# A decoder step on Trainium2: half of the fourth sequence's pages asked by ScalarE among the units, two tiles of x normed and turned one unit sooner

## The chip, the cores and the metric

The kernel runs on one core of one Trainium2 chip. The core's engines have instruction queues of their own: TensorE (PE in the profile) multiplies and transposes, VectorE (DVE) and ScalarE (ACT) work on tiles, GpSimd (POOL) does a little of the same, and SyncE (SP) here only asks for transfers. SP, ACT and POOL each ask for DMA transfers ("ask" in this document: the instruction that starts a transfer; "land": the moment its data is there). The metric is device microseconds of one execution, lower is better; the kernel before took 1262.57 us (median of three runs, 1260.37 to 1264.19).

## What is computed

One inference step of a one-layer decoder: forgetting attention (FoX) beside native sparse attention (NSA), gates, an output projection and an MLP, for a prompt of 512 tokens and for eight sequences of eight new tokens, each with a past of 2048 tokens in paged caches. The past of a sequence is 16 pages of 128 tokens, and a page table says where each lies. The change touches the part of NSA that compresses the past: raw keys and values of blocks of tokens go through a small MLP.

```python
def compress_blocks(x, pos, w1, w2):
    b, n = x.shape[:2]
    n_chunk = n // CMP_STRIDE
    xc = x[:, :n_chunk * CMP_STRIDE].reshape(b, n_chunk, CMP_STRIDE, NSA_GROUPS, HEAD_DIM)
    pos = pos.reshape(2, CMP_STRIDE, 1, HEAD_DIM)
    w1 = w1.reshape(2, CMP_STRIDE, HEAD_DIM, CMP_HIDDEN)
    lead = jnp.einsum('bncgd,cdh->bngh', xc + pos[0], w1[0])
    trail = jnp.einsum('bncgd,cdh->bngh', xc + pos[1], w1[1])
    return jnp.einsum('bngh,hd->bngd', jax.nn.silu(lead[:, :-1] + trail[:, 1:]), w2)
```

`x` here is a sequence's raw keys or values out of `cache_nsa_kv`. The change also moves the first step of the layer itself, `h = rms_norm(x, norm1_g) * (1 + sc1) + sh1`, for the first two tiles of 128 prompt tokens.

## The kernel before, in words

The change lies in `first_stage` (L509), the first 180 us or so of the step. It walks through 40 units. A unit is (sequences, `j` of 4, key or value): units 0 to 7 belong to sequence 0 alone, 8 to 15 to sequence 1 alone, 16 to 23 to sequences 2 and 3 together, 24 to 31 to 4 and 5, 32 to 39 to 6 and 7. A unit of one sequence is 256 columns wide, one of two is 512.

What a unit does: `cmp_order` copies a quarter of the sequence's pages (`cpg`) into another order (`ro`) on DVE, once for a key unit and the value unit behind it. The pages of a sequence lie in one tile, each spread over 16 of its 128 partitions and one half of their columns, so a `ro` copy (L115), which takes all partitions and both halves, reads all 16 pages, and the first one of a sequence can't start before the last page has landed. `rows_turn` turns `ro` on PE into `ct` (L83, four transposes for a sequence), and `split` brings `ct` back in two parts: `xh` by ACT (L112) and the remainder `xl` by DVE (L131). `cmp_hidden` is the matmuls `hid` on PE (L77), from `xh` and `xl` and the weights. The loop issues the turns of unit u+1 ahead of the matmuls of unit u; the order of PE's turns and matmuls is a fixed chain (`link`). Behind the matmuls of unit u follows whatever stands in `todo[u]`.

What stands in `todo` near the change: `norm(k)` squares tile k of x on ACT (`sq`), sums, and scales x on DVE (`norm_scaled`); `turned(k)`, two units later, turns the scaled tile on PE in two halves of four transposes (`nt`) and copies them into `hf`, one half by ACT and one by DVE. The constants' turns and the bias matmuls stand at units 10 and 12. x tiles are loaded by POOL into two buffers, the ada weights (`wada`, 1 MB each) by POOL too, from unit 13 on.

Who asks for the pages: `cmp_pages` asks for a sequence's pages on the queue named, through `by_page`: it reads eight entries of the page table into registers (L162), then issues eight asks of 128 KB each (L155), in the order 0, 4, 1, 5 and so on. SP asks for half of sequence 0 and ACT for the other half, SP then for all of 1, 2 and 3 ahead of the units, and for 4 to 7 out of `todo[8]`, `[14]`, `[20]` and `[22]`. Each ask is ordered behind the one before on its queue (`dma`), so the queue of an engine is first in, first out. `cpg` has four buffers, so sequence 4's pages go into the room of sequence 0.

The scheduler orders each engine's instructions by what they depend on. `pinned` and `behind` fix a piece of work behind the last `xh` copy and the last `xl` subtraction issued so far.

Of the kernel before, what the change touches and what calls it, by code (L numbers as in the profile page):

```python
# [45 lines left out]
class Step:  # L46
# [386 lines left out]

        self.cpg[b] = pe.tile([P, 2, 8, 256], F32, tag="cpg", bufs=4, name=f"cpg{b}")

    def cmp_pages(self, eng, b, pages=slice(0, 16), toks=slice(0, 8)):
        def load(p, n):
            page = self.I["cache_nsa_kv"][0, bass.ds(n, 1)].rearrange("o (q c) e g d -> (o q) c (e g d)", q=16)
            self.dma(eng, self.cpg[b].rearrange("(q p) h c e -> p q h c e", p=8)[p % 8, :, p // 8, toks],
                     page[:, toks, 0:256])  # L440

        self.by_page(eng, b, pages, load, 8, (0, 4, 1, 5, 2, 6, 3, 7))

    def cmp_order(self, pl, u):

# [63 lines left out]
    def first_stage(self, pl, pe, hf):  # L509
# [7 lines left out]
        def load_x():  # L517
            k = len(xs)
            xs.append(pe.tile([P, D], F32, tag="x", bufs=2, name=f"x{k}"))
            self.dma("gpsimd", xs[k][:TILES[k][1]], self.x_rows(k))  # L520

        def norm(k):
            with self.tc.issue_after(self.last_high):
                self.norm_scaled(xs[k], 0, k, xs[k], pl.tile([P, D], BF16, tag="csx", name=f"sq{k}"))

        def turned(k):
            t0, m = TILES[k]
            for h in range(2):
                self.copy(hf[:, 4 * h:4 * h + 4, t0:t0 + m], self.norm_turned(xs[k], 0, k, h))

        def behind():
            both = ExitStack()
            for i in (self.last_high, self.splits[-1]):
                both.enter_context(self.tc.issue_after(i))
            return both

        def pinned(f):
            def g():
                with behind():
                    f()  # L540
            return g
# [18 lines left out]
        self.constants()  # L560
        self.late_constants()
        self.cmp_pages("sync", 2)
        self.cmp_pages("sync", 3)

        ada, ends = [4, 0, 5, 1, 6, 2, 7, 3], {}
        todo = {u: [] for u in range(40)}
# [2 lines left out]
        todo[18] += [pinned(self.cmp_second_half)]  # L569
        todo[10] += [self.constants_turned, self.ada_turned, lambda: ends.update(b=self.cmp_bias(pe))]  # L570
        todo[12] += [lambda: self.cmp_bias_end(ends["b"])]
        for k, u in enumerate((12, 14, 17, 19, 23)):
            todo[u - 2] += [lambda k=k: norm(k)]
            todo[u] += [lambda k=k: turned(k)]
        pages = lambda b: lambda: (self.cmp_tile(pe, b), self.cmp_pages("sync", b))
        wada = lambda k: lambda: self.ada_first_load(pe, ada[k])
        def asked():
# [3 lines left out]
            with self.tc.issue_after(g.ins):  # L581
                load_x()

        todo[3] += [asked]
        todo[5] += [asked]
        todo[8] += [pages(4)]
# [1603 lines left out]
```

## Time and profile before

| | before |
|---|---|
| runs | 1262.57 us median (1260.37 to 1264.19) |
| profiled execution, its time | 1260.9 us |
| its span, first to last instruction | 1259.1 us |
| mean granted TensorE clock | 0.985 |
| up to the first turn of a page, at 18.0 us | PE idle |
| 18.0 to 172.0, the units | PE busy 145.0 of 154.0 us |
| 172.0 to 180.0, end of the units to the projection `z` | PE busy 6.3 of 8.0 us |
| behind 180.0 | PE busy 1049.3 of 1079.1 us |

The profile is of one execution; its times are microseconds from the first instruction. "Busy" is the union of an engine's compute instructions. A row of the timeline or of the chain begins with the start and the duration, then the engine, the line of the kernel, the operation, its result and source by the program's names with shapes, and in brackets the idle time before it and what ended it. A row of the windows shows for a stretch its length, the busy time and the number of instructions of PE, of PE's weight loads, of DVE, ACT and POOL, then the granted TensorE clock, the busy share of the DMA engines and GB/s. A row of the waits has the engine, what it waited to do, what it waited for, then the total, the number of times and the longest. "SPq" is SP's own instruction queue.

### The profile page before, as it was taken

How to read it: one execution, taken by the hardware profiler on the slowest of the kernel's cores; microseconds unless marked ns; L12 is line 12 of the kernel's file. 1: busy time of each engine (PE TensorE's matmuls, PEld its weight loads, DVE VectorE, ACT ScalarE, POOL GpSimd, SP SyncE). 2: the span in 40 equal slices, each digit the busy share in tenths (PEclk: the TensorE clock that was granted, in tenths of full speed). 3: DMA queues.
4: the chain of work that ended last, by engine and by line, in shares of the span. 5: the costliest groups of instructions: out<-in, count | busy, mean ns of one | idle time of the engine just before them, and what ended most of it. 6: DMA issues, size and time to landing. Idle time of an engine off the chain costs nothing.

```text
span 1259.1 us, 24790 instructions
## 1 busy us (share of the span) xinstructions
PE 1200.7 (95%) x9475; PEld 1030.0 (82%) x9475; DVE 695.4 (55%) x1893; ACT 509.4 (40%) x1136; POOL 130.3 (10%) x139
## 2 busy tenths in 40 slices
PE   4799999999999999999899998979999999999998
PEld 3787779999666656666899998979989889898896
DVE  3777775686788845655533345664233333434545
ACT  2444453444777744444422223254413123132230
POOL 2110000001211210000200000002102011020110
PEclk9999999999999899999999999999999999999999
DMA  9897337795766469885843324024304223142202
GB/s 208 230 250 200 109 97 249 249 320 177 252 222 206 146 201 321 254 272 179 223 115 85 85 84 131 4 68 134 101 34 134 68 68 100 39 129 68 67 18 75
DMA packets 170201, 188.11 MB, mean 149 GB/s; under 512 B 16185, under 2 KB 149762, under 8 KB 167906
## 3 DMA queue, kind: packets, MB, share of 16 engines
q1 hardware_dynamic: 157890, 167.13, 43.6%
q0 software_dynamic: 6880, 16.25, 4.5%
q10 hardware_dynamic: 5312, 3.15, 1.1%
q8 instruction: 75, 1.23, 0.4%
q14 instruction: 44, 0.36, 0.1%
HBM read 176.48 MB, written 30.90 MB: 165 GB/s over the span
## 4 chain that ended last, share of the span: by engine, by line
PE 83%; DVE 6%; DMA 4%; ACT 2%; SPq 2%; issue 1%; DVEq 0%; ACTq 0%
PE dn L77 17%; PE up L77 16%; PE z L77 9%; PE mg L77 8%; PE hid L77 5%; PE br L77 4%; PE ss L77 4%; PE wo L77 3%; SPq L155 2%; PE k L83 2%; DMA cpg<-in_cache_nsa_kv 2%; PE so L77 2%; PE ct L83 2%; PE ada L77 2%; PE sp L83 1%
## 5 line engine op out<-in xcount | busy, mean ns | idle before, releaser
L77 PE MATMUL z<-winh,h 128*128 128x264 f32 (+1 forms) x576 | 112.7, 289 | 1.9 <-DVE h L767 1.7
L1979 POOL TENSOR_TENSOR u<-u 128x576 f32<-128x576 f32 x32 | 54.7, 1711 | 428.7 <-ACT u L112 336.9
L77 PEld LDWEIGHTS z<-winh,h 128*128 128x128 f32 x576 | 93.0, 192 | 4.1 <-DVE h L767 2.9
L77 PE MATMUL z<-winl,h 128*128 128x264 f32 (+1 forms) x320 | 88.7, 286 | 0.0
L100 DVE TENSOR_TENSOR acc<-acc,dn 128x512 f32<-128x512 f32 x60 | 39.8, 686 | 77.4 <-PE dn L77 77.4
L77 PE MATMUL mg<-hH,wmh 128*128 128x288 f32 x256 | 76.6, 300 | 2.4 <-ACT wmh L112 2.4
L77 PE MATMUL mg<-hH,wml 128*128 128x288 f32 x256 | 75.8, 297 | 0.9 <-DVE wml L131 0.9
L77 PE MATMUL mg<-hL,wmh 128*128 128x288 f32 x256 | 72.6, 294 | 0.0
L112 ACT ACTIVATE xh<-ct 128x256 fp32r<-128x256 f32 x128 | 48.0, 384 | 57.9 <-PE ct L83 35.5
L767 DVE TENSOR_TENSOR u<-u,u 128x512 fp32r<-128x512 f32 x64 | 27.4, 469 | 63.0 <-ACT u L112 62.9
L77 PEld LDWEIGHTS z<-winl,h 128*128 128x128 f32 x320 | 61.2, 192 | 0.0
L131 DVE TENSOR_TENSOR xl<-ct,xh 128x256 fp32r<-128x256 f32 x128 | 51.4, 421 | 17.6 <-ACT xh L112 15.6
L83 PE MATMUL ct<-identF,ro 128*128 128x128 f32 x256 | 37.3, 286 | 20.5 <-DVE ro L115 19.8
L131 DVE TENSOR_TENSOR wml<-wmr,wmh 128x1024 fp32r<-128x1024 f32 x16 | 19.6, 1225 | 65.6 <-ACT wmh L112 65.6
L77 PEld LDWEIGHTS mg<-hH,wmh 128*128 128x128 f32 x256 | 48.6, 190 | 2.8 <-ACT wmh L112 2.7
L83 PEld LDWEIGHTS ct<-identF,ro 128*128 128x128 f32 x256 | 30.5, 149 | 23.8 <-DVE ro L115 18.4
L77 PEld LDWEIGHTS mg<-hH,wml 128*128 128x128 f32 x256 | 49.1, 192 | 1.1 <-DVE wml L131 1.1
L112 ACT ACTIVATE u<-up 128x256 f32<-128x256 f32 (+1 forms) x96 | 27.7, 325 | 50.9 <-PE up L77 50.9
L77 PEld LDWEIGHTS mg<-hL,wmh 128*128 128x128 f32 x256 | 47.1, 188 | 0.1
L77 PE MATMUL hid<-xh,w1hlv 128*128 128x512 f32 (+1 forms) x160 | 45.2, 369 | 0.5 <-ACT xh L112 0.4
L77 PE MATMUL hid<-xh,w1hlk 128*128 128x512 f32 (+1 forms) x160 | 45.0, 369 | 0.1
L112 ACT ACTIVATE u<-u 128x576 fp32r<-128x576 f32 x32 | 21.9, 686 | 44.2 <-POOL u L1979 44.2
(950 smaller groups left out, 3596.5 us busy)
## 6 DMA issues: line engine op xcount, KB each, us to landing
adw<-in_w_ada SPq DMA_DIRECT2D x16, 1024.0 KB
foxD<-in_cache_fox_kv SPq DMA_DIRECT2D x128, 128.0 KB
wur<-in_w_up SPq DMA_DIRECT2D x32, 512.0 KB
wdr<-in_w_down SPq DMA_DIRECT2D x32, 512.0 KB
cpg<-in_cache_nsa_kv SPq DMA_DIRECT2D x120, 128.0 KB
fr<-foxD SPq DMA_DIRECT2D x28, 512.0 KB
sr<-in_cache_nsa_kv SPq DMA_DIRECT2D x112, 128.0 KB
wada<-in_w_ada POOLq DMA_DIRECT2D x8, 1024.0 KB, 6.6
```

The source lines that it names most:

```text
L77: ins = self.nc.tensor.matmul(out, a, b, start=start, stop=stop, skip_group_check=True)
L83: ins = self.nc.tensor.transpose(out, in_, self.identF[:n, :n])
L100: self.nc.vector.tensor_tensor(out, a, b, op=op)
L112: return self.nc.scalar.activation(out, in_, f, **kw)
L131: self.splits.append((eng or self.nc.vector).tensor_tensor(l, x, h.bitcast(F32), op=OP.subtract).ins)
L155: self.issued[eng] = getattr(self.nc, eng).dma_start(out, in_).ins
L767: (eng or self.nc.vector).tensor_tensor(h2[:, o:o + n], x[:, i:i + n], h2[:, i:i + n].bitcast(F32), op=OP.subtract)
L1979: nc.gpsimd.tensor_tensor(u[j], u[j], u[j], op=OP.mult)
```

## The change

`cmp_pages` gets a parameter `step`, the number of table entries read at a time, with the old order of asks for 8 and the plain order otherwise. SP asks ahead of the units only for pages 0 to 7 of sequence 3 (the fourth). Pages 8 to 15 are asked by ACT, two each out of `todo[7]`, `[9]`, `[11]` and `[13]`, each pair with a table read of its own, and pinned behind the latest `xh` and `xl`. `norm` and `turned` of tiles 0 and 1 move from units 10/12 and 12/14 to 9/11 and 11/13.

```diff
-    def cmp_pages(self, eng, b, pages=slice(0, 16), toks=slice(0, 8)):
+    def cmp_pages(self, eng, b, pages=slice(0, 16), toks=slice(0, 8), step=8):
...
-        self.by_page(eng, b, pages, load, 8, (0, 4, 1, 5, 2, 6, 3, 7))
+        self.by_page(eng, b, pages, load, step, (0, 4, 1, 5, 2, 6, 3, 7) if step == 8 else None)
...
         self.cmp_pages("sync", 2)
-        self.cmp_pages("sync", 3)
+        self.cmp_pages("sync", 3, slice(0, 8))
...
-        for k, u in enumerate((12, 14, 17, 19, 23)):
+        for k, u in enumerate((11, 13, 17, 19, 23)):
             todo[u - 2] += [lambda k=k: norm(k)]
             todo[u] += [lambda k=k: turned(k)]
...
+        for k, u in enumerate((7, 9, 11, 13)):
+            todo[u] += [pinned(lambda k=k: self.cmp_pages("scalar", 3, slice(8 + 2 * k, 10 + 2 * k), step=2))]
         todo[3] += [asked]
```

In the built program ACT's four pairs stand behind the `xh` copies of units 8, 10, 12 and 14. The program's transfers between HBM and the core that SP and ACT ask for share eight completion counters in rotation.

## The prediction

> **What bounds the kernel now.** I read the page first, then who waited for whom on TensorE (PE), then the chain of waits around the longest wait inside the first stage, then the stretches of the clock.
>
> ```profile
> span 1259.1 us, 24790 instructions
> PE 1200.7 (95%) x9475; PEld 1030.0 (82%) x9475; DVE 695.4 (55%) x1893; ACT 509.4 (40%) x1136; POOL 130.3 (10%) x139
> ```
>
> ```profile
> PE nt L83 <- DVE x L104: 5.1, 1, 5.1
> PE z L77 <- DVE h L767: 1.7, 1, 1.7
> ```
>
> PE is busy for 95% of the span, so a change is worth what it takes from, or adds to, PE's idle time. In the stage that is edited one wait stands out: 5.1 us before the turns (transposes) of x tile 1.
>
> ```profile
> 54.62 5.03 DMA cpg<-in_cache_nsa_kv
> ...
> 60.64 0.69 DVE ro L115
> ...
> 62.72 1.97 PE nt L83 x8
> 64.68 1.71 PE ct L83 x8
> ```
>
> The chain gives the reason. The last of the 32 pages that SP asks for sequences 2 and 3 is asked at 54.62 and lands 5.03 us later. VectorE (DVE) stands in its program order at the reordering copy `ro` of that page, so the scaling of x tile 1 stands behind it until 62.7, and PE, done with its units, waits for that.
>
> ```profile
> 58.56:61.98 3.42, 0.00 (x0) 0.00 (x0) 2.10 (x7) 0.52 (x1) 0.00 (x0) 1.00 1.02 314
> 61.98:65.39 3.41, 2.67 (x13) 2.68 (x14) 1.35 (x3) 0.60 (x1) 0.41 (x1) 0.50 1.09 254
> 65.39:68.80 3.41, 3.41 (x18) 3.41 (x17) 1.63 (x5) 2.46 (x6) 1.04 (x2) 0.50 0.92 270
> ...
> 178.03:181.44 3.41, 1.59 (x8) 1.16 (x9) 3.35 (x9) 3.41 (x7) 0.76 (x3) 1.00 0.26 100
> 181.44:184.85 3.41, 3.41 (x15) 3.07 (x14) 3.41 (x11) 1.34 (x3) 0.00 (x0) 0.50 0.97 234
> ```
>
> The wait costs more than itself. After a stretch without a matmul the granted clock (third number from the end) is 0.50 for two stretches, 61.98 to 68.80; PE runs again from 62.72, so 6.08 us pass at half speed, a loss of 3.04. The wait and its tail together cost 8.1 us.
>
> **The change, part by part.** (1) SP asks for 8 pages fewer ahead of sequence 4. (2) ScalarE (ACT) asks for those 8 in four pairs, behind the copies of units 8, 10, 12 and 14, each pair with a read of the page table. (3) Tiles 0 and 1 are normed and turned one unit sooner. The number of copies, turns and matmuls stays. In the order of the built program the pairs stand in ACT's queue ahead of the next unit's `xh` copies, and the copies of two neighbouring units are interleaved behind some of them. The built order also swaps neighbours in later stages; no row prices that, I take 0, with 1 us either way in the range.
>
> What ACT pays for one pair: one table read and two asks, with what stands between them.
>
> ```profile
> 36.12 0.53 SPq L162
> ```
>
> ```profile
> L155 ACTq DMA_DIRECT2D cpg<-in_cache_nsa_kv x8: 546/547/670, 3.0 to 12.6; - x8
> ```
>
> A table read took 0.53 (on SP), an ask 0.55 on ACT. With what computes its address an ask takes 0.73: two of them fill SP's time from the end of that read, 36.65, to the end of the ask at 37.55 (below), 38.10. So a pair is 0.53 + 2 x 0.73 = 2.0 us in which ACT starts nothing behind it. But an ask also waits: HBM transfers of SP and ACT rotate through eight counters, and one is taken again only when its last transfer has landed.
>
> ```profile
> 3.88 6.29 DMA cpg<-in_cache_nsa_kv
> 10.19 4.77 DMA cpg<-in_cache_nsa_kv
> 14.98 7.60 DMA cpg<-in_cache_nsa_kv
> ```
>
> ```profile
> ACT w1hlk L112 <- DMA cpg<-in_cache_nsa_kv: 11.6, 1, 11.6
> ```
>
> Asked at 3.88, landed at 10.17, next ask on that counter at 10.19, and so on: this chain shows the rotation, and the last row shows that ACT's compute stands still behind its own asks (11.6 us at the start).
>
> *First pair.* By the built order its asks use the counters of the 8th and the 10th page of sequence 2. Those are asked at 34.68 and 37.55:
>
> ```profile
> 34.68 1.40 SPq L155
> ...
> 37.55 0.55 SPq L155
> ```
>
> ```profile
> w2rawk<-in_cmp_w_k POOLq DMA_DIRECT2D x1, 32.0 KB, 6.2
> bfox<-in_b_fox_f POOLq DMA_DIRECT2D x1, 4.0 KB, 5.3
> ```
>
> ```profile
> 39.56 0.38 ACT L112 ACTIVATE xh<-ct 128x256 fp32r<-128x256 f32 x1 [0.49 <-DVE xl L131]
> 40.56 0.39 ACT L112 ACTIVATE xh<-ct 128x256 fp32r<-128x256 f32 x1 [0.61 <-PE ct L83]
> ```
>
> ```profile
> 42.15 0.49 PE L77 MATMUL hid<-xh,w1hlv 128*128 128x256 f32 x2
> ```
>
> How long a page takes there is read from POOL's transfers of the same moment (34.0 to 37.2, while two x tiles load): 6.2 and 5.3 us. So the counters come free at about 40.9 and 42.8. ACT arrives at 39.6 (after unit 8's second copy), reads the table until 40.1, asks at 40.9, asks again at 42.8 and is through at 43.4. Unit 9's first copy starts then instead of at 40.56; its matmuls start at 43.8 instead of 42.15: 1.65, and the second copy, now behind one of unit 10, adds 0.45. I take 2.1 us of PE idle. Bounds: 0 (counters free on arrival: through at 41.6, copy done at 41.9) and 3.0 (another 0.9 of landing, as the 7.60 row allows). What waits behind ACT here is DVE's `xl` of unit 9 and PE's hidden matmuls.
>
> *Second pair.* Ahead of it stand the square of tile 0 (1.05, as that of tile 1 below) and ACT's tanh, for which I allow as much, some 2.2 us, so the copies of unit 11 come some 4.2 us after those of unit 10. PE has turns of the constants and the bias matmuls at this place, and the next chain of matmuls; I take 0, at most 0.6. Without that cover it would be about 3.
>
> ```profile
> 45.62 0.24 PE L83 MATMUL b<-identF,pos 32*128 32x32 f32 x1
> ...
> 48.67 0.66 PE L83 MATMUL ct<-identF,ro 128*128 128x128 f32 x4
> ```
>
> ```profile
> 52.90 1.05 ACT L112 ACTIVATE sq<-x 128x1024 bf16<-128x1024 f32 x1
> ...
> 55.30 0.39 ACT L112 ACTIVATE xh<-ct 128x256 fp32r<-128x256 f32 x1 [0.49 <-DVE xl L131]
> ```
>
> (45.62 to 48.67 is that cover, 3.05 us.) *Third pair.* Square of tile 1 (1.05), pair (2.0) and the copy of tile 0's turns, for which with the square's read I allow 0.8, lie together, 3.85 us. Against them PE has tile 0's turns, 1.0 (half of the 1.97 at half clock), and a unit, 2.0 (its two copies on ACT follow each other by 1.00, from 39.56 to 40.56): 0.9, between 0 and 1.5. *Fourth pair.* Covered by a unit and the turns of tile 1; for those turns, which wait for DVE's scaling, 0.6, between 0 and 1.2.
>
> *The last page.* All these only matter if nothing later hides them, and something does: the `ro` copy of sequence 3 waits for the 16th page, which is now ACT's. Unit 14's copies end at 55.69 before; with 2.1 + 0.9 they end at 58.7, the table read and the first ask end at 59.96, and the last page is asked at 60.0 instead of 54.62. At that time the engines are full: the next x tile and the first ada weights are asked as before.
>
> ```profile
> 54.19 0.54 POOL L155 DMA_DIRECT2D x<-in_x_prompt  x1 [16.20 <-DMA cpg<-in_cache_nsa_kv]
> 54.80 0.91 POOL L155 DMA_DIRECT2D wada<-in_w_ada  x1
> ```
>
> ```profile
> wada<-in_w_ada POOLq DMA_DIRECT2D x1, 1024.0 KB, 9.1
> ```
>
> From 54.2 on the engines owe 1.57 MB to POOL, nine pages to SP and four to ACT (13 x 0.131): 3.27 MB. The engines moved 227 GB/s from 53.00 to 58.56, and 314, 254 and 270 in the three stretches shown above:
>
> ```profile
> 53.00:58.56 5.56, 4.63 (x41) 4.43 (x38) 4.62 (x20) 3.77 (x10) 1.45 (x2) 1.00 0.74 227
> ```
>
> That is 0.99 MB by 58.56, 2.06 by 61.98, 2.93 by 65.39, and all at 66.7. Bounds: 65.0 (the 5.03 of the chain) and 69.1 (the 9.1 of `wada`). I take 67.5, 0.8 above the 66.7: the asks come 1.7 later still if the first pair's wait halves the clock, for which I give one chance in two. Then `ro` 0.69, and PE turns sequence 3's half of unit 16 at 68.2. Before, that half began at 65.5 (the second four of the eight at 64.68). So PE is 2.7 later there, whatever the pairs cost ahead of it. The rest of the old half-clock tail, (68.80 - 65.5)/2 = 1.65, is saved; but PE waits once more. Before, it was through with its units at 62.72 - 5.1 = 57.6; with tile 1's turns (1.0) and the pairs (2.1 + 0.9 + 0.6) it is ready at 62.2. So it has waited 5 to 6 us, and pays a tail again: 1.7 for one stretch, 3.0 as before for two; I take 2.5. **Sum: +2.7 - 1.65 + 2.5 = +3.55 us.** Of the waits of PE that follow in this stage the longest is `z` (1.7, for DVE), and none is for a page, so SP being free sooner wins nothing and the loss passes on whole.
>
> On the clock the row and a page differ. The stretch 178.03 to 181.44 still had 1.59 us of matmuls and the next one had half the clock. The Trainium skill ("TensorE: Matmul & The Clock Gate", "What's actually happening") says the gate falls after at least one idle window of some 3.4 us, free-running. By the row the first pair's 2.1 us can cost a tail of 1.7; by the rule it costs none. In the sum it would be hidden by the page's wait in both cases.
>
> The profiled execution took 1260.9 (span 1259.1 and 1.8 around it); with the sum 1264.4. The median of the runs shown is 1262.57, 1.7 above it; on that scale I forecast **1266.2 us**.
>
> **The rivals.** *ACT's pages are served in turn and land early.* At the start ACT's eight asks (3.0 to 12.6 in the row above) went through beside SP's, so a short queue need not stand behind a long one. If ACT gets a third of some 280 GB/s, its four pages need 5.6 us from about 57.5: the last lands at 63.3, PE turns sequence 3 at 64.2 instead of 65.5, and no stretch is idle enough for a tail: -1.3 - 1.65 = -2.95, **1259.6**. It decides where the last page lands by 64.5. Against it: POOL's megabytes kept the last page of before 5.03 us. The Trainium skill ("DMA: Bandwidth & Descriptors", "Queues, rings and completion order") has each engine go round its queues packet by packet, which would bring this out; no row here shows ACT's queue beside POOL's large loads.
>
> *The waits for counters repeat.* If the first and the third pair each halve the clock for a stretch (1.7 each) and the last page is asked at about 63.4, in the slack after POOL's load, it lands near 69.1: PE 4.3 later, -1.65, +3.0 and 1 for later stages, **1269.2**. For it: the row of 178.03. Against it: the waits are split into pieces of 0.2 to 1.6.
>
> *The change doesn't do what it says.* The last page lands when PE reaches unit 16 anyway, the pairs and the page's wait give 8 us in place of 8.1: **1262.6**.
>
> **How the numbers follow.** My forecast has 0.55, the early landing 0.20, the repeated waits 0.13, no effect 0.12. A measurement of this kernel tells about 0.3% (3.8 us) from no change. The forecast's own range, from landings at 65.0 to 69.1, is 1263.5 to 1268.5 and its middle lies at the edge of that: 0.30 slower, 0.24 same, 0.01 faster. The early landing is 0.11 faster (if the first pair finds its counters free too) and 0.09 same; the repeated waits are slower; no effect is 0.10 same and 0.02 slower. Together 0.12 faster, 0.43 same, 0.45 slower. The range reaches from the early landing, with 0.6 for the spread of runs, to the repeated waits with 0.8: 1259.0 to 1270.0.
>
> **What would show it.** In the profile of the changed kernel: the wait of `nt` for `x` under 1 us; a wait of PE `hid` for ACT `xh` of 1.5 to 2.5 near 43; a new wait of PE `ct` for DVE `ro` of 3 us or more near 64 to 68, with the DVE copy released by a `cpg` transfer asked on ACT's queue at about 60; a stretch at clock 0.50 behind it; and the `z` matmuls, which before begin in the stretch from 178.03, starting 3 to 4 us later. It is wrong if ACT's last page lands before 64.5, if ACT's first ask does not wait for a landing, or if the clock stays at 1.00 through the stage.

## The result, and the profile after

The changed kernel takes 1265.79 us (median of 20 runs, 1259.91 to 1271.81) against 1260.38 of the kernel before (20 runs, 1256.10 to 1265.07). The ratio is 1.0039, with an interval of 1.0024 to 1.0054: slower by 4.9 us. The execution that was profiled took 1262.44, the sixth lowest of its twenty.

First the page of the kernel after, as before its first two lines:

```profile
span 1260.7 us, 24792 instructions
PE 1199.8 (95%) x9475; PEld 1027.8 (82%) x9475; DVE 694.8 (55%) x1893; ACT 509.6 (40%) x1136; POOL 130.4 (10%) x139
```

Nothing here tells the two kernels apart. The view of PE's waits from 18 to 180 us does. Two of its rows before:

```profile
PE ct L83 <- DVE ro L115: 19.8, 2, 18.4
PE hid L77 <- ACT xh L112: 0.4, 1, 0.4
```

and after:

```profile
PE ct L83 <- DVE ro L115: 24.9, 4, 18.3
PE hid L77 <- ACT xh L112: 3.1, 3, 2.4
...
PE nt L83 <- DVE x L104: 0.4, 1, 0.4
```

The wait that the change is aimed at is gone: `nt` waits 0.4 us for x tile 1, against 5.1. In its place PE waits 3.1 for ACT's copies (0.4 before), and for `ro` 6.6 behind the first turn (24.9 less 18.3) where it was 1.5. The chain of waits says where, and who caused it:

```profile
37.43 6.00 DMA cpg<-in_cache_nsa_kv
...
43.45 0.56 ACTq L155
...
44.05 0.39 ACT xh L112
...
44.49 0.84 PE hid L77 x3
...
60.01 0.12 ACTq L162
...
60.34 0.56 ACTq L155
...
61.05 8.19 DMA cpg<-in_cache_nsa_kv
...
69.46 0.70 DVE ro L115
...
70.30 1.09 PE ct L83 x4
```

Read from the top: a page that SP asked for at 37.43 lands at 43.43; only then can ACT make its second ask, and only behind that does it copy `xh`, for which `hid` on PE stands. At the bottom ACT asks for the last page of sequence 3 at 61.05. It lands 8.19 us later, `ro` follows, and PE turns sequence 3 for unit 16 at 70.30. Before, that was at 65.5.

The windows show the clock around both places (columns as before):

```profile
42.77:46.19 3.42, 1.67 (x8) 1.15 (x9) 1.60 (x5) 1.92 (x5) 0.00 (x0) 1.00 0.68 200
46.19:49.60 3.41, 3.41 (x19) 3.41 (x18) 2.45 (x7) 2.19 (x5) 0.00 (x0) 0.50 0.79 220
63.25:66.67 3.42, 1.92 (x15) 1.50 (x14) 1.63 (x4) 2.34 (x5) 1.16 (x2) 1.00 1.07 274
66.67:70.08 3.41, 0.00 (x0) 0.00 (x0) 0.62 (x2) 0.08 (x1) 0.00 (x0) 1.00 1.06 273
70.08:73.49 3.41, 3.19 (x15) 3.22 (x16) 2.79 (x7) 1.88 (x4) 0.00 (x0) 0.50 1.05 322
```

Each long wait is followed by a stretch at 0.50. The sum of it stands at the first `z` matmul that waits, in the timeline of PE before:

```profile
179.65 0.39 PE L77 MATMUL z<-winh,h 128*128 128x264 f32 x1 [1.68 <-DVE h L767]
```

and after:

```profile
184.65 0.39 PE L77 MATMUL z<-winh,h 128*128 128x264 f32 x1 [1.68 <-DVE h L769]
```

The edited stage lost 5.0 us, which is what the runs show for the whole kernel. Why the profiled execution is only 1.5 us longer lies far behind the edit. Near 602 us PE waits for ACT's copy of the merge gates' weights (view of its waits from 590 to 620), before:

```profile
PE mg L77 <- ACT wmh L112: 2.4, 1, 2.4
```

and after:

```profile
PE mg L77 <- ACT wmh L112: 1.0, 1, 1.0
```

The windows there, before:

```profile
601.28:604.70 3.42, 1.54 (x8) 1.16 (x9) 1.93 (x6) 2.23 (x5) 3.15 (x6) 1.00 1.15 264
604.70:608.11 3.41, 3.41 (x44) 3.24 (x44) 1.40 (x3) 2.20 (x7) 3.18 (x6) 0.50 1.07 240
```

and after:

```profile
602.56:605.97 3.41, 2.43 (x45) 1.42 (x41) 1.10 (x4) 1.34 (x2) 0.93 (x2) 1.00 1.13 260
605.97:609.39 3.42, 2.56 (x46) 2.14 (x46) 1.83 (x7) 2.23 (x8) 3.42 (x8) 1.00 1.13 247
```

Before, the idle time fell mostly into one stretch and the next ran at half clock; in this execution of the kernel after, the wait is 1.4 us shorter, it is split over two stretches and no stretch is halved, which is 1.7 us more (half of 3.41). Together that is 3 of the 5 us. The 20 runs, 4.9 us slower, do not keep that gain, so the edited stage, not the span of one execution, is what to compare below.

### The profile page after: what moved, and what is told of

The parts are those of the page before. It is cut to its first block, busy times and chain, and to the rows that moved or that the text cites. A ratio compares the mean times of both kernels' runs of the same rounds, so it can differ in the third digit from the quotient of the medians.

```text
span 1260.7 us, 24792 instructions
## 1 busy us (share of the span) xinstructions
PE 1199.8 (95%) x9475; PEld 1027.8 (82%) x9475; DVE 694.8 (55%) x1893; ACT 509.6 (40%) x1136; POOL 130.4 (10%) x139
## 4 chain that ended last, share of the span: by engine, by line
PE 86%; DVE 5%; DMA 4%; ACT 2%; SPq 1%; issue 1%; ACTq 0%; DVEq 0%
PE dn L77 17%; PE up L77 16%; PE z L77 9%; PE mg L77 8%; PE hid L77 5%; PE br L77 4%; PE wo L77 4%; PE ss L77 4%; DMA cpg<-in_cache_nsa_kv 3%; PE k L83 2%; PE ct L83 2%; PE so L77 2%; PE ada L77 2%; PE sp L83 1%; SPq L155 1%; PE sfox L77 1%
## 5 line engine op out<-in xcount | busy, mean ns | idle before, releaser
L83 PE MATMUL ct<-identF,ro 128*128 128x128 f32 x256 | 37.0, 284 | 25.6 <-DVE ro L115 24.9
L83 PEld LDWEIGHTS ct<-identF,ro 128*128 128x128 f32 x256 | 29.9, 147 | 29.2 <-DVE ro L115 18.3
```

The source lines that it names most:

```text
L83: ins = self.nc.tensor.transpose(out, in_, self.identF[:n, :n])
```

## The experiments

The ratio is to the kernel before, from runs on the same chip in turn. "z" is the start of the `z` matmul above (179.65 before, 184.65 after); the first turn of a page starts between 18.2 and 18.8 in all these profiles, so differences of 0.5 in z say nothing. z too is of one execution. It says where a kernel won or lost; how much, the runs say, and the two differ by up to 4 us: e2 loses 7.7 us by its runs (0.0061 of 1260) and 3.9 by z, e10 wins 2.5 and loses 0.9, e6 wins 1.6 and loses 1.4. e1 to e4, e5 to e8 and e9 to e11 ran on three different chips.

| run | what differs from the kernel before | ratio | interval | z |
|---|---|---|---|---|
| the change | both parts | 1.0039 | 1.0024 to 1.0054 | 184.65 |
| e1 | shift of tiles 0 and 1 | 0.9988 | 0.9971 to 1.0006 | 178.98 |
| e2 | pages by ACT | 1.0061 | 1.0039 to 1.0082 | 183.54 |
| e3 | the change, pairs four units sooner | 1.0014 | 0.9997 to 1.0032 | 182.25 |
| e4 | the change, `wada` later | 1.0011 | 0.9991 to 1.0030 | 181.97 |
| e5 | shift, `wada` later | 0.9949 | 0.9929 to 0.9970 | 175.05 |
| e6 | shift of tile 1 alone | 0.9987 | 0.9962 to 1.0013 | 181.04 |
| e7 | shift, pages by POOL | 0.9961 | 0.9942 to 0.9981 | 175.48 |
| e8 | shift of tile 1 alone, `wada` later | 0.9967 | 0.9946 to 0.9988 | 175.66 |
| e9 | shift, pages by POOL, `wada` later | 0.9965 | 0.9948 to 0.9981 | 175.96 |
| e10 | `wada` later | 0.9980 | 0.9962 to 0.9998 | 180.51 |
| e11 | shift, `wada` later, one pair by ACT | 0.9990 | 0.9975 to 1.0005 | 177.11 |

**The two parts alone.** e1 has the shift without ACT's pages, against the kernel before:

```diff
-        for k, u in enumerate((12, 14, 17, 19, 23)):
+        for k, u in enumerate((11, 13, 17, 19, 23)):
```

> SP asks for all 16 pages of sequence 3 as before; only the norm and the turns of tiles 0 and 1 move one unit. Theory (the loss comes from the page that ACT asks last at 61.05 and that lands at 69.24): no wait of nt for x over 1 us, no wait of hid for xh near 43, the last page lands near 59.7 and PE turns sequence 3's half of unit 16 near 61.5 to 62.5 instead of 65.1; z starts 3 to 4.5 us sooner than at 179.65; 3 to 5 us faster than before (ratio 0.996 to 0.998). Rival (the shift itself costs, or DVE stays in front of the page in any case): ratio 1.000 to 1.003.

e2 is the changed kernel with that line as it was before.

> ACT asks for pages 8 to 15 of sequence 3 as in the change; norm and turns stay where they were. Theory: the wait of hid for xh near 43 (2 to 3 us) and the wait for ACT's last page are there as with the change; the page lands within 1.5 us of 69.2; 4 to 7 us slower than before (ratio 1.003 to 1.0055). Rival (the shift is what costs): ratio 0.999 to 1.001.

e2 came out on the side of the theory, a little above its range: 1.0061. So the pages cost, and the shift does not. But e1 won far less than expected. `nt` waits 1.5 us and `hid` only 0.5 for `xh`, and still sequence 3 is turned only 0.6 us sooner (64.86 against 65.5). Two lines of PE's timeline of e1:

```profile
61.40 0.63 PE L83 MATMUL ct<-identF,ro 128*128 128x128 f32 x4 [1.16 <-DVE ro L115]
64.86 1.08 PE L83 MATMUL ct<-identF,ro 128*128 128x128 f32 x4 [2.83 <-DVE ro L115]
```

The first is sequence 2, the second sequence 3, whose last page lands near 64 though SP asks for it at 55.0, nearly when it did before. POOL's timeline of e1 has a reason:

```profile
52.11 0.54 POOL L155 DMA_DIRECT2D x<-in_x_prompt  x1 [13.94 <-PE nt L83]
52.72 0.91 POOL L155 DMA_DIRECT2D wada<-in_w_ada  x1
```

Tile 0 is turned a unit sooner, its buffer comes free sooner, and 1.5 MB of x and ada weights are asked 2.1 us sooner than before, now ahead of the last pages. That was put to the test twice, by taking the megabyte away from there and by leaving tile 0 where it was.

**The megabyte.** e5 is e1 with the first load of ada weights behind the next x tile; e4 is the changed kernel with the same edit:

```diff
-        todo[13] += [wada(0)]
-        todo[14] += [pages(5), load_x]
+        todo[14] += [pages(5), load_x, wada(0)]
```

> Only the shift (SP asks for all pages), and the first megabyte of ada weights behind the next x tile. Theory (with the shift alone tile 0 is turned sooner, its buffer comes free 2.1 us sooner, POOL's loads start at 52.1 instead of 54.2 and push the last page of sequence 3 from 59.6 to 63.6): without the megabyte the last page lands at 58 to 60.5, PE waits for it under 2 us, no half clock there; z starts 3 to 5 us sooner than at 179.65; 2.5 to 5 us faster than before (ratio 0.996 to 0.998). Rival (the page lands late for another reason, SP's own asks): it lands after 62.5, ratio as with the shift alone (0.998 to 1.000).

> The whole change, but POOL loads the first megabyte of ada weights behind the next x tile, about 6 us later. Theory (the 8.19 us of the last page are its share of full DMA engines): it lands 2 to 4 us sooner, at 65 to 67, and z starts 2 to 3 us sooner than at 184.65; 1 to 4 us slower than before (ratio 1.001 to 1.003). Rival (what stands ahead of it is ACT's and SP's own queue): it lands as before, within 1 us of 69.2, ratio 1.003 to 1.005. A wait of ada for wada of over 1 us would be a new cost and is read apart.

e5 has the lowest ratio of all, 0.9949, below what was expected, with z 4.6 us sooner than before. By the records of its completion counter the last page of sequence 3 lands at 58.3 (asked at 54.2); in e1, where only the megabyte is earlier, at 63.6. One turn of eight, both sequences together, is left of the two waits above, in PE's timeline of e5:

```profile
61.01 1.22 PE L83 MATMUL ct<-identF,ro 128*128 128x128 f32 x8 [1.50 <-DVE ro L115]
```

In e4 the last page is asked at nearly the same time as in the changed kernel. The chain of waits of e4:

```profile
60.82 5.83 DMA cpg<-in_cache_nsa_kv
...
66.87 0.70 DVE ro L115
...
67.71 0.63 PE ct L83 x4
```

5.83 us in place of 8.19: the page lands 2.6 us sooner, PE turns sequence 3 2.6 sooner (67.71 against 70.30) and z starts 2.7 sooner, within the expectation. So the landing of that page decides the end of the stage, and about a third of its time was the megabyte.

**Leaving tile 0 where it was.** e6 moves tile 1 alone, e8 adds the late megabyte:

```diff
-        for k, u in enumerate((12, 14, 17, 19, 23)):
+        for k, u in enumerate((12, 13, 17, 19, 23)):
```

> Only tile 1's norm and turns move one unit; tile 0 stays, so its buffer is freed when it was before. Theory: x and the ada weights are asked within 0.6 us of 54.2 and 54.8, the last page of sequence 3 lands at 59 to 61, PE turns sequence 3's half of unit 16 at 61 to 62.5 and z starts 2.5 to 4.5 us sooner than before; ratio 0.9965 to 0.998. Rival (the time at which tile 0 frees its buffer does not matter): the page lands near 63.6 and the ratio is that of the shift alone.

> Tile 1 alone one unit sooner and the first megabyte of ada weights behind the next x tile. Theory: the last page lands by 59.5, PE waits for it under 1.5 us, z 3.5 to 5 us sooner than before; ratio 0.996 to 0.9975, within 0.001 of the shift with the late megabyte. Rival: the megabyte, 7 us later, makes ada wait for wada over 2 us and gives it back; ratio 0.998 or more.

e6 went against the theory as it was put, and its ratio is the rival's, that of the shift alone. POOL asks when it did before (first line, from POOL's timeline of e6),

```profile
54.65 0.91 POOL L155 DMA_DIRECT2D wada<-in_w_ada  x1
```

and yet the page lands late, by the chain of e6:

```profile
56.05 8.45 DMA cpg<-in_cache_nsa_kv
...
64.89 0.70 DVE ro L115
```

The difference is on SP: its last ask for sequence 3 comes at 56.05 here, 1.40 us behind the megabyte; in the kernel before it came at 54.62, 0.18 ahead of it (54.80), and took 5.03 instead of 8.45. So what counts is not the time at which tile 0 frees its buffer by itself, but which of the two asks comes first; before, that hung on 0.18 us. e6's edit leaves SP's asks alone; why they come later in this execution is not shown. With the megabyte out of the way (e8) the gain is there, 0.9967, as expected, though 0.0018 and not 0.001 from e5. The wait of `ada` that the rival feared is in none of the views of e4, e5, e8 or e9.

**The megabyte without the shift.** e10 is the kernel before with the edit of e5's `wada` alone.

> The kernel before with the first megabyte of ada weights behind the next x tile, nothing else. Theory (before, the last page was asked 0.18 us ahead of that megabyte and so did not stand behind it; tile 1's scaling stands behind the page on DVE in any case): the page lands at 57.5 to 59.5, nt still waits 3 to 5 us for x, z 0 to 2.5 us sooner than 179.65; ratio 0.998 to 1.000. Rival (the late megabyte alone is the gain of the shift with the late megabyte): z 3.5 us sooner or more, ratio under 0.997.

The ratio, 0.9980, lies in the range, but its profile is not the one described: DVE's `ro` copies for sequence 3's page begin at 61.84, and `nt` waits longer than before, not less (the view of PE's waits of e10):

```profile
PE nt L83 <- DVE x L104: 6.7, 1, 6.7
```

z is later too, 0.9. The page came late without the megabyte: SP asks for it at 55.4, 1.0 us behind the next x tile (54.34), where before it was 0.4 behind (54.62 and 54.19). So the half megabyte of x may delay it as well; no run takes that apart. The runs are 0.2% faster than before, and so is the profiled execution (1258.44), but not in the edited stage; where the gain comes from is not shown. What the profile does show is that without the shift tile 1 stays behind the page on DVE.

**What ACT's asking costs.** e4 and e5 differ only in who asks for the 8 pages, and lie at 1.0011 and 0.9949: 0.62% or 7.8 us for ACT's four pairs, the late asking of the last page included (z 6.9). Two runs take that apart. e11 is e5 with one pair by ACT and the other 14 pages by SP:

```diff
-        self.cmp_pages("sync", 3)
+        self.cmp_pages("sync", 3, slice(0, 8))
+        self.cmp_pages("sync", 3, slice(10, 16), step=6)
...
+        for k, u in enumerate((7,)):
```

> The shift with the late megabyte, and of sequence 3 ACT asks one pair only (pages 8 and 9, behind unit 8's copies); SP asks the other 14, so no page is late. Theory (ACT standing at a counter costs PE by itself what hid waits for xh, and a half-clock stretch with it): hid waits 1.7 to 2.5 us for xh near 43, z 2 to 4 us later than the 175.05 without the pair; ratio 0.997 to 0.9985. Rival (that wait is hidden in what follows): z within 1 us of 175.05, ratio under 0.9965.

In e11 `hid` waits once for 0.99 and once for 0.4, no stretch is halved there, and z is 2.1 later than in e5:

```profile
43.02 0.51 PE L77 MATMUL hid<-xh,w1hlv 128*128 128x256 f32 x2 [0.99 <-ACT xh L112]
```

One pair is not hidden by what follows: the rival is out. The wait is smaller than the theory said; the unit's matmuls behind it take 2.3 us where they take 1.5 in e5, and that with the wait makes up most of the 2.1. The runs put the pair at 0.41% (0.9990 against 0.9949), 5 us, more than z shows; the two intervals together leave room for 2, and against e9, from the same chip, it is 0.25%. The rest isn't settled.

e3 is the changed kernel with all pairs four units sooner:

```diff
-        for k, u in enumerate((7, 9, 11, 13)):
+        for k, u in enumerate((3, 5, 7, 9)):
```

> The whole change, but ACT's four pairs four units sooner (behind units 3, 5, 7, 9). Theory (the late landing costs, the counters' waits are hidden in it): the last page is asked near 50 and lands by 57, PE does not wait for it; what stays are ACT's waits for counters, 2 to 4 us in all; sequence 3's half of unit 16 is turned at 61 to 63; 1 to 4 us faster than before (ratio 0.997 to 0.999). Rival (ACT standing at counters is the loss in itself): each of four pairs costs PE 2 us or more, 2 us slower than before or worse (ratio over 1.0015).

Its ratio lies between the two ranges. It holds the shift too, so what the pairs cost is read against e5 and e7, which have the same shift and no late page: z is 7.2 and 6.8 us later, 1.7 to 1.8 us for each pair. The last page no longer holds PE up, but the second and third pair do. PE's timeline of e3:

```profile
41.25 0.63 PE L83 MATMUL ct<-identF,ro 128*128 128x128 f32 x4 [3.52 <-DVE ro L115]
...
48.50 0.51 PE L77 MATMUL hid<-xh,w1hlv 128*128 128x256 f32 x2 [1.33 <-ACT xh L112]
```

The first wait was 1.5 before; the `ro` copy is pinned behind `xh`, and ACT stood 2.9 us at the second pair (to 37.90). Behind it the stretch from 42.02 to 45.43 is at 0.50. The third pair's wait is in the chain of e3:

```profile
31.52 7.88 DMA cpg<-in_cache_nsa_kv
39.42 7.14 DMA cpg<-in_cache_nsa_kv
...
46.58 0.56 ACTq L155
...
47.31 0.71 ACTq L155
```

An ACT page asked at 31.52 lands at 39.40; SP takes its counter again at 39.42, for a page that lands at 46.56. ACT is through with its copies at 43.18, comes to its third pair and asks at 46.58: some 3 us at a counter that SP had taken before ACT came, and PE with it. Asking sooner did not help, because the counters are no freer there. The rival's point, ACT's standing as a loss in itself, holds, and its price of 2 us for each pair is near what the comparison gives (by the runs 8.2 us for the four against e5, 6.7 against e7).

**A queue that nobody computes on.** e7 asks for the 8 pages on POOL in one go; e9 adds the late megabyte:

```diff
+                              "gpsimd": mybir.EngineType.Pool}
...
+        todo[7] += [pinned(lambda: self.cmp_pages("gpsimd", 3, slice(8, 16)))]
```

> The change with its shift, but the 8 pages are asked by POOL's queue in one go behind unit 8's copies (one table read), so ACT asks for nothing among the units and POOL's small loads, the next x tile and the ada weights come behind the pages. Theory (what the change loses is ACT standing at counters, then the late last page): no wait of hid for xh over 0.6, the last page of sequence 3 lands by 57, PE does not wait for it; z starts 4 to 7 us sooner than at 179.65; ratio 0.994 to 0.9975. Rival (pages asked on a second queue only share full engines): the last page lands after 60 and the ratio is 0.998 or more. A new wait could come from the small loads behind the pages (w2raw, gains), which then land 6 to 10 us later.

> The 8 pages on POOL's queue, the shift, and the first megabyte of ada weights behind the next x tile. Theory (once the last page lands by 60 nothing more is to be had there, the rest of PE's waits is DVE's chain): z starts within 1 us of the 175.05 of the shift with the late megabyte; ratio 0.9935 to 0.9965. Rival (the page still binds there): z 2 us sooner or more, ratio under 0.9935.

Moving the pages off SP does what the change set out to do once the asking engine has no copies to make: 0.9961 and 0.9965, z 4.2 and 3.7 sooner than before. `hid` waits 0.4 and 0.5 for `xh`, as before, and sequence 3 is turned right behind sequence 2. PE's timeline of e7:

```profile
61.23 0.63 PE L83 MATMUL ct<-identF,ro 128*128 128x128 f32 x4 [1.16 <-DVE ro L115]
62.02 0.63 PE L83 MATMUL ct<-identF,ro 128*128 128x128 f32 x4 [0.16 <-DVE ro L115]
```

The late megabyte adds nothing here; POOL asks for the pages ahead of it. e5, e7 and e9 agree within their intervals. In e5 SP still asks for all pages, so the gain is that of the shift once no page is late; that moving pages off SP adds to it, no run shows. What is left of PE's waits at unit 16 is 1.3 to 1.6 us for `ro` copies, most of it behind other work on DVE.

## Why the prediction was right, and where its sizes were off

The forecast was 3.55 us slower; the runs say 4.9 and z 5.0. The mechanism was right: the wait of `nt` goes, ACT stands at counters, its last page lands late and PE waits for it at unit 16. That the time itself, 1266.2, lies 0.4 from the measured 1265.79 is partly luck: it was counted from three runs of the kernel before with a median of 1262.57, the twenty have 1260.38, and this 2.2 too much makes up for a loss taken too small. By its steps:

- *The wait of `nt` goes.* Under 1 us was forecast, 0.4 came. The shift by itself takes it to 1.5 (e1 and e5), and is worth 4.6 us of z as soon as nothing lands late (e5). It is not the only way: in e2, without the shift, it is 0.9, because DVE scales x at 60.53 there, ahead of the `ro` copy of the late page (68.39).
- *First pair.* ACT was to ask at 40.9 and 42.8 and be through at 43.4; it asked at 42.15 and 43.45 and was through at 44.0, and `hid` waited 2.4 where 2.1 was forecast. The chain names the cause that was forecast, a counter held by the tenth page of sequence 2 (37.43). The halved clock behind it, given one chance in two, came (46.19 to 49.60).
- *The other pairs.* 0, 0.9 and 0.6 forecast. Of the 3.1 of `hid`'s waits 2.4 lie at the first pair and 0.4 ahead of all pairs, as before; 0.3 is left for the third, where 0.9 was forecast, and `nt` waits 0.4. A table read on ACT takes 0.50, near the 0.53 borrowed from SP, but the last one runs beside the copy ahead of it, and only 0.12 of it stands in the chain.
- *The last page.* This term was mis-sized. Forecast: asked at 60.0, landing at 67.5, PE 2.7 later at sequence 3. Measured: asked at 61.05, landing at 69.24, just past the upper bound of 69.1, PE 4.8 later (70.30 against 65.5). The estimate served all bytes that were owed at the measured rate and allowed 0.8 for one chance in two of a late ask. The ask came 1.05 later than forecast, which the halved clock is large enough to explain, and the page took 8.19. e4 shows that 2.4 of these were the megabyte ahead of it. The forecast also had the x tile and that megabyte asked as before (54.19 and 54.80); POOL asks for them at 56.42 and 57.04 in the kernel after, so the bytes that it counted from 54.2 on came later.
- *The tails.* 1.65 saved, 2.5 paid again was forecast. One stretch was halved, 70.08 to 73.49, and PE ran in 3.19 of it: 1.6. The 2.5 lay between the price of one such stretch and of two. With measured sizes the sum is +4.8 - 1.65 + 1.6 = +4.75, against 5.0 at z.
- *What hides the pairs.* The forecast said that the early waits vanish in the page's wait. For the changed kernel that holds: when e4 took 2.4 off the page, z followed at once (2.7), so the page and not ACT's stand set the time. It would have been wrong to read from it that ACT's stands are free: with no late page the pairs show in z (e11, and e3 against e5).
- *The later stages.* 0 was taken, with 1 us either way. From 180 to 597 us PE stays near 5 us behind (the last turns of `sr`, 592.5 before, begin at 597.3 after), so the swapped neighbours cost nothing up to there. What followed is the shorter wait and the clock near 602.

Of the rivals, no effect is out, and the early landing did not come: the page landed at 69.24, not by 64.5. The Trainium skill ("DMA: Bandwidth & Descriptors", "Queues, rings and completion order") lets each engine go round its queues packet by packet. Taken alone, that would let a short queue overtake POOL's; e6, with 8.45 us for a page of SP asked 1.40 us behind the megabyte, speaks against counting on it. The repeated waits came in part: the landing near 69.1 and one halved stretch at the first pair, but no second one at the third, no ask as late as 63.4 and no tail of 3.0.

## What to carry to other kernels

An ask is not free for the engine that makes it: it can stand for a completion counter that another queue took, and everything in that engine's program order stands with it. Here the same pages cost least on a queue whose engine has no copies to make, SP (e5) or POOL (e7). When a load comes early because a buffer comes free early, look at what it now stands ahead of; here one megabyte, asked a few microseconds sooner or later, decided 3.9 us of TensorE (z of e1 against e5). And one profiled execution can be off by a halved stretch far from the edit: compare the start of the next stage, and let many runs judge the whole.

## What was not expected of the hardware

- Order against a large load matters: a 128 KB page asked 0.18 us ahead of a 1 MB load took 5.03 us, one asked 1.40 us behind it 8.45 (kernel before and e6; one page each).
- The page that an ask stands for can be another queue's: in e3 ACT stood some 3 us for a counter that SP had taken at 39.42, 0.02 us after it came free and well before ACT came to ask.
- A half-idle stretch can be enough for the half clock: 1.67 us of matmuls in 3.42 (42.77 to 46.19), and the next stretch is at 0.50; with 1.92 (63.25 to 66.67) the next one is still at 1.00. This is no threshold: in the kernel before, 423.79 to 427.20 has 2.26 us of matmuls, and the stretch behind it is at 0.50 too. The Trainium skill ("TensorE: Matmul & The Clock Gate", "What's actually happening") asks for at least one idle window of some 3.4 us; the first of these stretches differs from that, and the measurement counts here.
